# Strassen's products in a channel mixer's gate and up projections, and the down projection's weight sums computed earlier

## The chip, the cores and the metric

The kernel runs on one core of a Trainium2 chip. A core has a matrix engine (PE, with its weight loads shown apart as PEld), three engines for elementwise work (DVE, the vector engine; ACT, the scalar engine, which computes activation functions; POOL, GpSimd) and SP, which here only issues transfers. Each engine runs its own list of instructions strictly in order and waits on semaphores for the others. The metric is the device time of one execution in microseconds (us); the kernel before takes 1001.63 us in the median of three runs (1001.45 to 1002.13).

## The reference

The kernel is one layer of a streaming encoder block on x of 512 tokens by 1024 channels, in float32:

```python
h = rmsnorm(x, norm1_w)
proj = h @ w_in                       # q, k, v, z, b, a, glu, gates
o = gated_delta_rule_chunked(q, k, v, g, beta)
out_a = (rmsnorm(o, dn_norm_w) * silu(z)) @ dn_w_o
c = silu(layernorm(causal_depthwise_conv(glu_a * sigmoid(glu_b), cm_dw_w) + cm_dw_b))
out_b = c @ cm_w_pw2 + cm_b_pw2
x = x + (gate_a * out_a + gate_b * out_b) @ w_out
h2 = rmsnorm(x, norm2_w)
f_gate, f_up = split(h2 @ ffn_w_gate_up)      # 1024 -> 2 x 2816
x = x + (silu(f_gate) * f_up) @ ffn_w_down    # 2816 -> 1024
return rmsnorm(x, norm_f_w)
```

The change is in the last five lines, the channel mixer, and in the two output projections before it (`dn_w_o`, `cm_w_pw2`, then `w_out`).

## The kernel before, in words

**Split products.** To hold float32 accuracy on PE, every matrix is held as a high part (rounded to PE's float32r type) and a low part (the rest), and every product is three matmuls: high x high, high x low, low x high. `unit` loads 128 x 1024 weights (`raw`) on SP's queue, ACT makes the high part (`whi`, L102) and DVE the low part by a subtraction (`wlo`, L104). All three tiles have three buffers. `split3` issues the three matmuls (L113), `col_tile` one column tile of 128 outputs over all 512 tokens: 8 blocks of the inner dimension x 3 matmuls of 512 columns.

**Order.** A scheduler lays each engine's instructions out from the program text, the engines' modelled costs and the buffers that come free; what results is one fixed list for each engine.

**Output projections.** After the mixers, `ln_mean` (L560 to 573) makes the layer norm's variance sum: ACT squares eight tiles and POOL adds them up in `sacc` (L572, seven additions); `ln_norm` (L575) multiplies that sum by a matrix of ones on PE (L577) and goes on from there. The eight column tiles of `dn_w_o` run around it, `ln_norm` standing behind the third, then the eight of `cm_w_pw2`, then `tok_mm` for `w_out`, whose end is the second norm (`norm2`: ACT squares, POOL adds and takes the root, L786 and L788; DVE scales; PE transposes into `hh` and `hl`, the split activations).

**Gate and up.** For each of 22 hidden tiles f, `col_tile` runs twice (gate, up), ACT takes Silu (L871), DVE multiplies (`fm`, L878). For f < 11 POOL also runs `sums(f)` (L850): it loads a 128 x 4 x 512 piece of the down weights on its own queue, makes Strassen's four weight sums (L854 to L857) in place and stores them to DRAM (`wsum`). The activations' sums for the down projection are made by DVE at L888 to L892.

**Down projection.** It is already Strassen's (in Winograd's form): seven products of halves, in three calls of `two` (11 steps of 12 matmuls) and a last single product (L981 to L1006), whose weights are split by `unit` in groups of two; the final norm's work (`norm_f`) is issued between the third call and the last product.

## Time and profile before

One profiled execution took 998.75 us, 997.0 us of it from the first to the last instruction.

| | |
|---|---|
| median of three runs | 1001.63 us |
| profiled execution, its span | 998.75 us, 997.0 us |
| mean granted PE clock | 0.989 of full |
| PE, DVE, ACT, POOL busy | 96%, 68%, 52%, 29% of the span |
| output projections up to the second norm | about 476 to 640 us |
| gate and up | about 633 to 875 us |
| down projection and final norm | 875 to 997 us |

How the views are read. A row of groups gives line, engine, operation, tiles written and read, the shape and the count, then busy time, mean nanoseconds of one, and the idle time before them with what ended it. A row of the timeline gives start and length in us, and in brackets how long its engine had idled and for whom. A row of the table by stage gives a stretch, its length, and for each engine its busy time and instructions, then PE's granted clock, the share of time that the DMA engines were busy and GB/s. A row of the chain of waits gives start, length and what stood on it. Matmuls are pipelined: the length of one in the records is longer than the distance between two starts, which is what counts for throughput.

### The profile page before, as it was taken

Reading aid. Unit: us, or ns where it says so; the run is one execution under the profiler, and the core shown is the slowest. Engines: PE = TensorE matmul, PEld = TensorE weight load, DVE = VectorE, ACT = ScalarE, POOL = GpSimd, SP = SyncE. Lnnn points to the kernel's source line nnn. Section 1 sums busy time; section 2 is a strip of 40 time slices with the busy share of each in tenths; the row PEclk is TensorE's granted clock in tenths of the full one; section 3 lists DMA queues with packets and bytes.
Section 4 is the critical chain, followed back from the end, with each engine's and each line's share of the span. In section 5 each row is a group of like instructions: output and inputs, shape, how many; then the busy total and the mean of one; then the engine's idle time right before and its main releaser. Section 6 shows DMA issues by size and latency. Waiting matters only on the chain.

```text
span 997.0 us, 13416 instructions
## 1 busy us (share of the span) xinstructions
PE 961.6 (96%) x4775; PEld 791.6 (79%) x4775; DVE 673.7 (68%) x1044; ACT 515.4 (52%) x1057; POOL 292.6 (29%) x410
## 2 busy tenths in 40 slices
PE   7999799999999999999999999999999999999995
PEld 5687678788878888888888888888888888888784
DVE  4879699898779759898486644643444554468963
ACT  6697477777868675543456322422222222356543
POOL 0323845265452542000040000144342432001412
PEclk9999899999999999999999999999999999999997
DMA  9233313223142131233844432356656565256462
GB/s 318 85 114 97 98 54 106 80 74 105 43 118 76 59 102 64 85 128 137 273 128 156 137 120 85 119 210 220 231 179 239 195 232 183 92 168 190 158 212 85
DMA packets 48291, 138.50 MB, mean 139 GB/s; under 512 B 7472, under 2 KB 9424, under 8 KB 45408
## 3 DMA queue, kind: packets, MB, share of 16 engines
q1 hardware_dynamic: 44016, 112.36, 34.1%
q0 software_dynamic: 3488, 24.17, 6.9%
q10 hardware_dynamic: 720, 1.11, 0.3%
q8 instruction: 37, 0.61, 0.3%
q14 instruction: 30, 0.25, 0.1%
HBM read 119.52 MB, written 18.10 MB: 138 GB/s over the span
## 4 chain that ended last, share of the span: by engine, by line
PE 82%; DVE 6%; ACT 4%; POOL 4%; issue 2%; DMA 1%; SPq 0%; POOLq 0%; ACTq 0%; DVEq 0%
PE mm L113 62%; PE w L113 11%; DVE cv L543 2%; DVE wlo L104 1%; POOL Un L349 1%; PE b L414 1%; PE g L312 1%; ACT whi L102 1%; PE sp L487 1%; PE g L345 1%; ACT Un L348 1%; PE b L420 1%; PE st L494 1%; PE st L482 1%; PE b L438 1%
## 5 line engine op out<-in xcount | busy, mean ns | idle before, releaser
L102 ACT ACTIVATE whi<-raw 128x1024 fp32r<-128x1024 f32 x167 | 176.4, 1057 | 315.5 <-PE mm L113 180.5
L113 PE MATMUL mm<-hh,whi 128*128 128x512 f32 x816 | 327.5, 402 | 0.0
L113 PE MATMUL mm<-hl,whi 128*128 128x512 f32 x816 | 322.4, 395 | 2.3 <-POOL hl L228 1.6
L113 PE MATMUL mm<-hh,wlo 128*128 128x512 f32 x816 | 322.0, 395 | 0.7 <-DVE wlo L104 0.7
L104 DVE TENSOR_TENSOR wlo<-raw,whi 128x1024 fp32r<-128x1024 f32 x167 | 218.1, 1306 | 115.1 <-ACT whi L102 114.3
L543 DVE SCALAR_TENSOR_TENSOR cv<-c,c31w,cv 128x512 f32<-128x512 f32 x240 | 179.7, 771 | 2.0
L113 PEld LDWEIGHTS mm<-hl,whi 128*128 128x128 f32 x816 | 154.1, 189 | 33.1 <-POOL hl L228 2.9
L113 PEld LDWEIGHTS mm<-hh,wlo 128*128 128x128 f32 x816 | 154.0, 189 | 32.2 <-DVE wlo L104 1.1
L113 PEld LDWEIGHTS mm<-hh,whi 128*128 128x128 f32 x816 | 154.2, 189 | 29.9 <-ACT hh L227 0.2
L375 POOL TENSOR_TENSOR ytm<-U,y 128x60 f32<-128x60 f32 (+14 forms) x120 | 51.0, 425 | 62.1 <-DMA U<-sc 44.7
L299 DVE SCALAR_TENSOR_TENSOR acc<-mm,c4w,acc 128x511 f32<-128x511 f32 (+2 forms) x72 | 53.2, 740 | 9.9 <-ACT acc L296 9.2
L878 DVE TENSOR_TENSOR fm<-mm,fsg 128x512 f32<-128x512 f32 x21 | 14.5, 691 | 65.7 <-PE mm L113 65.7
L377 POOL TENSOR_TENSOR y<-y,ytm 128x60 f32<-128x60 f32 (+14 forms) x120 | 50.9, 424 | 9.3
L113 PE MATMUL mm<-yh,whi 128*128 128x512 f32 x128 | 50.6, 396 | 0.0
L113 PE MATMUL mm<-yh,wlo 128*128 128x512 f32 x128 | 49.8, 389 | 0.0
L113 PE MATMUL mm<-yl,whi 128*128 128x512 f32 x128 | 49.8, 389 | 0.0
L113 PE MATMUL w<-whi,fh 128*128 128x512 f32 (+1 forms) x115 | 45.3, 395 | 2.8 <-ACT whi L102 2.8
L113 PE MATMUL w<-wlo,fh 128*128 128x512 f32 (+1 forms) x115 | 45.6, 397 | 2.4 <-DVE wlo L104 2.4
L113 PE MATMUL w<-whi,fl 128*128 128x512 f32 (+1 forms) x115 | 45.0, 393 | 0.0
L786 POOL TENSOR_SCALAR ss<-ss 128x1 f32<-128x1 f32 x17 | 5.7, 336 | 128.8 <-ACT sg L784 116.2
L339 POOL TENSOR_TENSOR ss<-ss,root 128x4 f32<-128x4 f32 x8 | 10.3, 1291 | 85.5 <-DVE ss L337 85.5
L915 POOL TENSOR_TENSOR A<-A,u 128x512 f32<-128x512 f32 x4 | 6.2, 1574 | 97.1 <-ACT u L946 70.6
(288 smaller groups left out, 1511.2 us busy)
## 6 DMA issues: line engine op xcount, KB each, us to landing
raw<-in_win_dram SPq DMA_DIRECT2D x61, 512.0 KB, 3.3
raw<-in_wgu_dram SPq DMA_DIRECT2D x44, 512.0 KB, 3.4
wst<-in_wdn_dram POOLq DMA_DIRECT2D x11, 1024.0 KB, 6.0
wsum<-wst POOLq DMA_DIRECT2D x11, 1024.0 KB, 4.9
raw<-wsum SPq DMA_DIRECT2D x44, 256.0 KB, 3.4
raw<-in_wdn_dram SPq DMA_DIRECT2D x33, 256.0 KB, 2.9
A<-in_x_dram SPq DMA_DIRECT2D x8, 512.0 KB, 6.8
U<-sc SPq DMA_DIRECT2D x64, 64.0 KB, 3.1
```

What stands on the lines that cost most here:

```text
L102: marked(S.activation(hi[:, 0:n], raw[:, 0:n], AF.Copy), "unit")
L104: marked(V.tensor_tensor(out=lo[:, 0:n], in0=raw[:, 0:n], in1=hi[:, 0:n].bitcast(F32), op=ALU.subtract), "unit")
L113: marked(PE.matmul(ps, l, r, start=first and i == 0, stop=last and i == 2))
L299: marked(V.scalar_tensor_tensor(out=acc[:, s:], in0=ps[:, :T - s], scalar=c4w[:, j, k:k + 1], in1=acc[:, s:], op0=ALU.mult, op1=ALU.add))
L312: PE.transpose(ps[:, n, :], src[:, n, :], ident)
L339: G.tensor_tensor(out=nk, in0=kk, in1=root4, op=ALU.pow)
L345: PE.matmul(ps[:, n, :], kT[:, n, :], kT[:, n, :], start=True, stop=True)
L348: S.activation(Un[:, n, :], ps[:, n, :], AF.Copy, scale=nb2[:, n:n + 1])
L375: G.tensor_tensor(out=tm[:, :, 0:w], in0=U[:, k, :, k + 1:], in1=y[:, :, k:k + 1].broadcast_to([P, NT, w]), op=ALU.mult)
L377: G.tensor_tensor(out=y[:, :, k + 1:], in0=y[:, :, k + 1:], in1=tm[:, :, 0:w], op=ALU.add)
L543: V.scalar_tensor_tensor(out=acc, in0=c[:, k:k + T], scalar=c31w[:, i, k:k + 1], in1=acc, op0=ALU.mult, op1=ALU.add)
L878: V.tensor_tensor(out=fm, in0=pu, in1=sg, op=ALU.mult)
```

## The change

**Gate and up by Strassen's seven products.** The first two hidden tiles stay as they are. For each further one, `pair(f)` takes the gate and the up column tile together as a 2 x 2 block matrix (inner dimension in halves, gate and up the other way) against the activations in halves of inner dimension and tokens. It runs seven products of 4 x 3 = 12 matmuls of 256 columns. Besides the products of w = [a11, a12] as loaded, and of a22 (`w22`), it needs the sums s3 = a11 - a21, a22 := a21 + a22, a11 := a22 - a11, a12 := a12 - a11, all made by POOL, the last three in place in the loaded tiles `ra` and `rb`. `ws` is the split of the changed `ra`, `w3` that of s3, `w1` that of the changed a22. The outputs are put together from the four PSUM tiles z by DVE (`u`, `v`, `cw`, `fm`). The activations' sums are made once. `operands(f)` makes the down projection's operands; two subtractions of it go from DVE to POOL.

**Weight sums earlier.** The generator `sums` works in halves of 256 columns with two buffers, a step behind each column tile of the output projections and in `tok_mm`, the rest ahead of the end of that stage.

**What goes with it.** y1 is stored to DRAM and loaded again for the down projection (`ysp`, `y2`), the hidden tiles from 11 on are spilled to DRAM (`spill`) and loaded again in `set_3`. The sets of the down projection are made two steps later in `two`, and the final norm's work is spread between the steps of the last product.

```diff
     ...
+    def wsplit(raw, pool=None):
+
+        n = raw.shape[-1]
+        hi, lo = ((pool or wp).tile([P, n if pool else 1024], F32R, name=x)[:, 0:n] for x in ("whi", "wlo"))
+        marked(S.activation(hi, raw, AF.Copy), "unit")
+        marked(V.tensor_tensor(out=lo, in0=raw, in1=hi.bitcast(F32), op=ALU.subtract), "unit")
+        return hi, lo
+
 ...
+    FK = FF // 2
+    wsum = [dram.tile([P, 4, T], F32, name="wsum", bufs=FK) for _ in range(FK)]
+
+    def sums():
+        for k in range(FK):
+            for c in (slice(0, T // 2), slice(T // 2, T)):
+                r = sp2.tile([P, 4, T // 2], F32, name="wst")
+                nc.gpsimd.dma_start(r, a["wdn"][k].rearrange("p (i c) -> p i c", i=4)[:, :, c])
+                b11, b12, b21, b22 = (r[:, i, :] for i in range(4))
+                G.tensor_tensor(out=b11, in0=b12, in1=b11, op=ALU.subtract)
+                G.tensor_tensor(out=b12, in0=b22, in1=b12, op=ALU.subtract)
+                G.tensor_tensor(out=b22, in0=b22, in1=b11, op=ALU.subtract)
+                G.tensor_tensor(out=b21, in0=b22, in1=b21, op=ALU.subtract)
+                nc.gpsimd.dma_start(wsum[k][:, :, c], r)
+                yield
+
+    summing = sums()
 ...
         col_tile(ps, a["wo"][j], oh, ol)
+        next(summing, None)
         ma = mp.tile([P, T], F32, name="ma", bufs=KD + 1)
 ...
         col_tile(ps, a["wpw"][j], yh, yl)
+        next(summing, None)
         mb = tp.tile([P, T], F32, name="acc4")
 ...
                 for n in range(NT):
                     part(n, kp2, w)
+                next(summing, None)
 ...
         if hf:
+            nc.scalar.dma_start(ysp[n], y1[:, n, :])
 ...
     tok_mm("wout", KD, mh, ml, norm2, transposes)
+    for _ in summing:
+        pass
 ...
-    def sums(k):
-        r = fp.tile([P, 4, T], F32, name="wst", bufs=1)
-        nc.gpsimd.dma_start(r, a["wdn"][k].rearrange("p (i c) -> p i c", i=4))
-        b11, b12, b21, b22 = (r[:, i, :] for i in range(4))
-        G.tensor_tensor(out=b11, in0=b12, in1=b11, op=ALU.subtract)
-        G.tensor_tensor(out=b12, in0=b22, in1=b12, op=ALU.subtract)
-        G.tensor_tensor(out=b22, in0=b22, in1=b11, op=ALU.subtract)
-        G.tensor_tensor(out=b21, in0=b22, in1=b21, op=ALU.subtract)
-        nc.gpsimd.dma_start(wsum[k], r)
 ...
+    def sub(out, in0, in1, eng=G, op=ALU.subtract):
+        eng.tensor_tensor(out=out, in0=in0, in1=in1, op=op)
 ...
+    def operands(f):
+        if f < FK:
+            set1.append(xset())
+            hi, lo = (t[:, t1] for t in set1[f])
+            xsplit(hi, lo, fms[f][:, t1])
+            return
+        b, fm = fms[f - FK], fms[f]
+        s1 = fq.tile([P, TH], F32, name="s1")
+        sub(s1, b[:, t2], fm[:, t2], V, ALU.add)
+        hi, lo = (t[:, t2] for t in set1[f - FK])
+        xsplit(hi, lo, s1)
+        sub(b[:, t2], b[:, t1], b[:, t2])
+        sub(b[:, t1], s1, b[:, t1])
+    def spill(f):
+        spills.append(dram.tile([P, T], F32, name="fsp", bufs=FK))
+        nc.scalar.dma_start(spills[-1], fms[f])
 ...
+    xb = {}
+    for i, (ks, ts, eng) in enumerate(((kl, t1, V), (kl, t2, V), (kh, t2, G), (kh, t1, G))):
+        xb[i] = fx.tile([P, KH, TH], F32, name="xb%d" % i)
+        sub(xb[i], hh[:, ks, ts].bitcast(F32), hl[:, ks, ts].bitcast(F32), eng, ALU.add)
+    b11, b12, b22, b21 = (xb[i] for i in range(4))
+    sub(b11, b12, b11, V)
+    sub(b12, b22, b12, G)
+    sub(b22, b22, b11, V)
+    sub(b21, b21, b22, V)
+    T2, T3, T4 = ([fq.tile([P, KH, TH], F32R, name="%s%d" % (n, i), bufs=1) for n in ("th", "tl")] for i in range(3))
+    xsplit(*T4, b21)
+    xsplit(*T2, b22)
+    xsplit(*T3, b12)
+    B11, B21, B22 = ([t[:, ks, ts] for t in (hh, hl)] for ks, ts in ((kl, t1), (kh, t1), (kh, t2)))
+    T1 = [t[:, kl, t2] for t in (hh, hl)]
+    def hprod(ps, w, i, x):
+        for k in range(KH):
+            s = slice(i * T + k * P, i * T + k * P + P)
+            split3(ps, (w[0][:, s], w[1][:, s]), x[0][:, k, :], x[1][:, k, :], k == 0, k == KH - 1)
+    def pair(f):
+        ra = wp.tile([P, 1024], F32, name="raw")
+        rb = we.tile([P, 1024], F32, name="raw")
+        nc.sync.dma_start(ra, a["wgu"][f])
+        nc.sync.dma_start(rb, a["wgu"][FF + f])
+        z = [bank() for _ in range(4)] if f % 2 == 0 else [bank(), bank2(), bank2(), bank2()]
+        w = wsplit(ra)
+        w22 = wsplit(rb[:, T:], we)
+        hprod(z[0][:, t1], w, 0, B11)
+        hprod(z[1][:, t1], w, 1, B21)
+        hprod(z[2][:, t1], w22, 0, T4)
+        a11, a12, a21, a22 = (r[:, i * T:i * T + T] for r in (ra, rb) for i in range(2))
+        s3 = we.tile([P, T], F32, name="s3", bufs=1)
+        sub(s3, a11, a21)
+        sub(a22, a21, a22, G, ALU.add)
+        sub(a11, a22, a11)
+        sub(a12, a12, a11)
+        ws = wsplit(ra)
+        hprod(z[0][:, t2], ws, 0, T2)
+        cw = fq.tile([P, T], F32, name="cw")
+        S.copy(out=cw[:, t1], in_=z[0][:, t1])
+        u = fq.tile([P, TH], F32, name="cu")
+        sub(u, cw[:, t1], z[0][:, t2], V, ALU.add)
+        hprod(z[1][:, t2], ws, 1, B22)
+        w3 = wsplit(s3, we)
+        hprod(z[3][:, t1], w3, 0, T3)
+        v = fq.tile([P, TH], F32, name="cv2")
+        sub(v, u, z[3][:, t1], V, ALU.add)
+        w1 = wsplit(rb[:, T:])
+        if f == 2:
+            xsplit(*T1, b11)
+        hprod(z[2][:, t2], w1, 0, T1)
+        sub(cw[:, t2], u, z[2][:, t2], V, ALU.add)
+        fm = hidden(f)
+        sub(fm.rearrange("p (i t) -> p i t", i=2), z[2].rearrange("p (i t) -> p i t", i=2),
+            v.rearrange("p (a t) -> p a t", a=1).broadcast_to([P, 2, TH]), V, ALU.add)
+        sub(cw, cw, z[1], V, ALU.add)
+        S.activation(cw, cw, AF.Silu)
+        sub(fm, fm, cw, V, ALU.mult)
+    ff = None
+    for f in range(2, FF):
+        pair(f)
+        if f - 1 >= FK:
+            spill(f - 1)
+        if ff is None:
+            fxs.close()
+            ff = ctx.enter_context(tc.tile_pool(name="ff", bufs=1))
+            operands(0)
+            operands(1)
+        operands(f)
+    spill(FF - 1)
 ...
-        fm = fp.tile([P, T], F32, name="fm", bufs=FF)
-        fms.append(fm)
-        V.tensor_tensor(out=fm, in0=pu, in1=sg, op=ALU.mult)
-        if f < FK:
-            sums(f)
-            set1.append(xset())
-            hi, lo = (t[:, t1] for t in set1[f])
-            xsplit(hi, lo, fm[:, t1])
-        else:
-            b = fms[f - FK]
-            s1 = fp.tile([P, TH], F32, name="s1")
-            V.tensor_tensor(out=s1, in0=b[:, t2], in1=fm[:, t2], op=ALU.add)
-            hi, lo = (t[:, t2] for t in set1[f - FK])
-            xsplit(hi, lo, s1)
-            V.tensor_tensor(out=b[:, t2], in0=b[:, t1], in1=b[:, t2], op=ALU.subtract)
-            V.tensor_tensor(out=b[:, t1], in0=s1, in1=b[:, t1], op=ALU.subtract)
 ...
+            if k > 1:
+                then(k - 2)
+        then(FK - 2)
+        then(FK - 1)
+    def set_2(k):
+        set2.append(xset())
+        xsplit(*set2[k], fms[k])
+    def set_3(k):
+        r = dp.tile([P, T], F32, name="rl", bufs=3)
+        nc.gpsimd.dma_start(r, spills[k])
+        set3.append(xset())
+        xsplit(*set3[k], r)
+        sub(fms[k][:, t1], r[:, t1], fms[k][:, t1])
 ...
+        if k < 2:
+            add(2 + k, c1, p4[k], op=ALU.subtract)
+            squares(0, 2 + k, c1)
+            squares(1, 2 + k, c2, True)
+        elif k < 4:
+            add(k - 2, c1, p2[k - 2])
+            for cs, eng in ((c1, nc.scalar), (c2, nc.sync)):
+                scaled_out(k, cs, eng)
+            first_half(k - 2)
```

The orders on the engines change in three places.

On DVE in gate-up, before (two hidden tiles; names carry buffer numbers, `wlo` with its `raw` and `whi` is a unit's low part, `fsg` the Silu, `fl` an operand's low part):

```order
L104 TENSOR_TENSOR wlo_6509<-raw_6505,whi_6507 128x1024
L878 TENSOR_TENSOR fm_6458<-mm_6395,fsg_6426 128x512
L104 TENSOR_TENSOR wlo_6554<-raw_6550,whi_6552 128x1024
L844 TENSOR_TENSOR fl_6468<-fm_6458,fh_6467 128x256
L104 TENSOR_TENSOR wlo_6586<-raw_6582,whi_6584 128x1024
L878 TENSOR_TENSOR fm_6535<-mm_6472,fsg_6503 128x512
```

And now, one pair. `raw_7043` and `raw_7044` are ra and rb of a pair n+1, `raw_7176` and `raw_7177` those of pair n+2, `cu_6985`, `cv2_7015`, `cw_6983`, `fm_7034` belong to pair n:

```order
L99 TENSOR_TENSOR wlo_7101<-raw_7043,whi_7100 128x1024
L886 TENSOR_TENSOR cv2_7015<-cu_6985,mm_6917 128x256
L886 TENSOR_TENSOR cw_6983<-cu_6985,mm_6916 128x256
L886 TENSOR_TENSOR fm_7034<-mm_6916,cv2_7015 128x512
L886 TENSOR_TENSOR cw_6983<-cw_6983,mm_6915 128x512
L99 TENSOR_TENSOR wlo_7133<-s3_7095,whi_7132 128x512
L99 TENSOR_TENSOR wlo_7151<-raw_7044,whi_7150 128x512
L886 TENSOR_TENSOR fm_7034<-fm_7034,cw_6983 128x512
L99 TENSOR_TENSOR wlo_7185<-raw_7176,whi_7184 128x1024
L883 TENSOR_TENSOR fl_7040<-fm_7034,fh_7039 128x256
L99 TENSOR_TENSOR wlo_7189<-raw_7177,whi_7188 128x512
L886 TENSOR_TENSOR cu_7118<-cw_7116,w_7047 128x256
```

Where DVE had three or four instructions for a tile, it now has twelve, and `ws` of pair n+1 (first row) stands ahead of the closing sums of pair n, and w22 of pair n+2 behind them.

On POOL in gate-up, before (one tile's weight sums between their transfers):

```order
L852 DMA wst_6306<-in_wdn_dram 128x2048
L854 TENSOR_TENSOR wst_6306<-wst_6306 128x512
L855 TENSOR_TENSOR wst_6306<-wst_6306 128x512
L856 TENSOR_TENSOR wst_6306<-wst_6306 128x512
L857 TENSOR_TENSOR wst_6306<-wst_6306 128x512
L858 DMA wsum_6167<-wst_6306 128x2048
```

And now (hidden tiles from 11 on; in each pair s3, two operand subtractions in fm, then a22, a11, a12):

```order
L886 TENSOR_TENSOR s3_8169<-raw_8117,raw_8118 128x512
L886 TENSOR_TENSOR fm_6471<-fm_6471 128x256
L886 TENSOR_TENSOR fm_6471<-s1_7974,fm_6471 128x256
L886 TENSOR_TENSOR raw_8118<-raw_8118 128x512
L886 TENSOR_TENSOR raw_8117<-raw_8118,raw_8117 128x512
L886 TENSOR_TENSOR raw_8117<-raw_8117 128x512
```

The four 512-column subtractions that no engine waited for in this stage are gone; the four in their place stand between a load and a split that PE waits for. The subtraction into `raw_8118` (a22) waits for DVE's low part of w22, which reads that place.

On POOL at the layer norm in the output projections, before:

```order
L736 DMA nw2_5419<-in_n2w_dram 128x1024
L572 TENSOR_TENSOR sacc_5012<-sacc_5012,acc4_5016 128x512
L572 TENSOR_TENSOR sacc_5012<-sacc_5012,acc4_5020 128x512
L572 TENSOR_TENSOR sacc_5012<-sacc_5012,acc4_5024 128x512
L572 TENSOR_TENSOR sacc_5012<-sacc_5012,acc4_5028 128x512
```

And now (`wst_5324` and `wst_5366` are the fifth and the sixth half of the weight sums):

```order
L734 DMA wsum_5063<-wst_5324 512x1x256
L730 TENSOR_TENSOR wst_5366<-wst_5366 128x256
L578 TENSOR_TENSOR sacc_5015<-sacc_5015,acc4_5019 128x512
L731 TENSOR_TENSOR wst_5366<-wst_5366 128x256
L578 TENSOR_TENSOR sacc_5015<-sacc_5015,acc4_5023 128x512
L732 TENSOR_TENSOR wst_5366<-wst_5366 128x256
L578 TENSOR_TENSOR sacc_5015<-sacc_5015,acc4_5027 128x512
L733 TENSOR_TENSOR wst_5366<-wst_5366 128x256
L578 TENSOR_TENSOR sacc_5015<-sacc_5015,acc4_5031 128x512
L734 DMA wsum_5063<-wst_5366 512x1x256
L578 TENSOR_TENSOR sacc_5015<-sacc_5015,acc4_5035 128x512
L728 DMA wst_5408<-in_wdn_dram 128x4x256
```

Ahead of the first row stand the five halves' loads, sums and stores; the weight sums are now woven into the seven additions. On PE the ones-matmul of `ln_norm` keeps its place.

More of the change, by code (lines that the diff above doesn't have):

```diff
@@ L750, in block_kernel @@
         V.tensor_tensor(out=ml[j], in0=mb, in1=mh[j].bitcast(F32), op=ALU.subtract)
+    ysp = [dram.tile([P, D], F32, name="ysp", bufs=NT) for _ in range(NT)]
     def tok_mm(wname, kts, xh, xl, post, between):
@@ L869, in block_kernel @@
             k_loop(*first[0], slice(2 * P, T))
-        sg = fp.tile([P, T], F32, name="fsg")
+        sg = fq.tile([P, T], F32, name="cw")
         S.activation(sg, pg, AF.Silu)
@@ L895, in block_kernel @@
+    ff = None
[10 more added lines that the diff above has]
+    spill(FF - 1)
+    fqs.close()
     hps.close()
     dp = ctx.enter_context(tc.tile_pool(name="dp", bufs=2, side="right"))
+    nfw = dp.tile([P, D], F32, name="nfw", bufs=1)
+    nc.gpsimd.dma_start(nfw, a["nfw"].partition_broadcast(P))
@@ L914, in add @@
     def add(n, cs, what, op=ALU.add, eng=V):
[L915 removed]
+        eng.tensor_tensor(out=y2[:, n, cs], in0=y2[:, n, cs], in1=what, op=op)
     def prods(w, i, x, j, accs, first, last):
@@ L1005, in block_kernel @@
         add(1, cs, ps)
-        norm_f(4 if c else 1, 1, cs)
+        squares(4 if c else 1, 1, cs, c)
+        if not c:
+            out(0)
+    out(1)
 def _layout(i):
```

119 lines of the change are left out of this document (58 added, 61 removed).

## The prediction

> **What bounds the kernel now.** I read the page's busy times first, then the table by stage, then the chain of waits.
>
> ```profile
> PE 961.6 (96%) x4775; PEld 791.6 (79%) x4775; DVE 673.7 (68%) x1044; ACT 515.4 (52%) x1057; POOL 292.6 (29%) x410
> ```
> ```profile
> core 0: us, PE busy (x) PEld busy (x) DVE busy (x) ACT busy (x) POOL busy (x), PEclk, DMA share, GB/s
> 476.00:516.00 40.00, 40.00 (x175) 32.27 (x174) 25.88 (x27) 20.26 (x30) 13.03 (x8) 1.00 0.63 212
> 516.00:587.00 71.00, 71.00 (x315) 58.76 (x314) 45.82 (x57) 31.17 (x40) 0.00 (x0) 1.00 0.46 144
> 647.20:700.00 52.80, 52.80 (x234) 43.72 (x233) 19.86 (x20) 14.55 (x20) 21.69 (x18) 1.00 0.62 216
> ```
> ```profile
> 647.16 228.28 PE mm L113 x1007
> ```
>
> In the output projections (476 to 587) and in gate-up (647.2 to 875.4) PE is busy all the time at full clock, DVE and POOL are not. The chain holds gate-up as one unbroken run of matmuls: 228.28 us / 1007 = 0.2267 us for a 512-column matmul, so 48 x 0.2267 = 10.88 us for one pair of column tiles. Whatever the change does, time there is gained only by less PE work, and lost once another engine needs over 10.88 us per pair.
>
> **Part 1, the matmuls.** Each of 20 pairs goes from 48 matmuls of 512 columns to 7 x 12 = 84 of 256. The program before has 256-column matmuls at the end of the norm:
>
> ```profile
> 642.08 0.28 PE L113 MATMUL w<-hh,whi 128*128 128x256 f32 x1
> ...
> 644.00 0.28 PE L113 MATMUL w<-hl,whi 128*128 128x256 f32 x1
> ```
>
> Sixteen starts lie between these two: 1.92 / 16 = 0.120 us, a little over half of 0.2267. So a pair is 84 x 0.120 = 10.08 us of PE. All that PE can give is 20 x 0.80 = 16 us.
>
> **Part 2, who feeds these products.** Prices of the other engines, alone:
>
> ```profile
> 647.27 0.69 DVE L878 TENSOR_TENSOR fm<-w,fsg 128x512 f32<-128x512 f32 x1 [0.58 <-PE w L113]
> 648.17 1.23 DVE L104 TENSOR_TENSOR wlo<-raw,whi 128x1024 fp32r<-128x1024 f32 x1 [0.21 <-ACT whi L102]
> 649.32 0.42 DVE L844 TENSOR_TENSOR fl<-fm,fh 128x256 fp32r<-128x256 f32 x1
> ```
> ```profile
> 650.37 1.29 POOL L854 TENSOR_TENSOR wst<-wst 128x512 f32<-128x512 f32 x1 [8.25 <-DMA wst<-in_wdn_dram]
> 651.73 1.29 POOL L855 TENSOR_TENSOR wst<-wst 128x512 f32<-128x512 f32 x1
> ```
> ```profile
> L102 ACT ACTIVATE whi<-raw 128x1024 fp32r<-128x1024 f32 x166 | 175.9, 1060 | 315.5 <-PE mm L113 180.5 <-issue 89.0 <-PE w L113 36.9
> ```
>
> DVE: 1.23, 0.69 and 0.42 us for 1024, 512 and 256 columns; one starts 0.08 before the record of the last ends (649.32 against 648.17 + 1.23), which makes 1.15, 0.62 and 0.35 from start to start. POOL: 1.29 us for 512 columns, 1.36 from start to start. ACT: 1.06 us for a 1024-column split.
>
> The orders shown above close a ring in which each link waits for the one before, once per pair. From the start of DVE's low part of the summed weights (ws) of pair n+1: ws 1.15; u+z3 and the two gate halves 0.35 + 0.35; fm 0.62; cw 0.62; low part of s3 0.62, of the last weight quarter 0.62; the product fm x cw 0.62; low part of w of pair n+2 1.15; fl 0.35; low part of w22 of pair n+2 0.69 with its end. That is 7.1 us. Only then may POOL overwrite a22, because w22 was split from that place; a22, a11, a12 are 3 x 1.36 = 4.1. Then ACT splits the sum (1.06), and DVE may start the next ws: 7.1 + 4.1 + 1.06 and some 0.1 of handing over = 12.4 us. Behind the waiting ws stand on DVE the closing sums of pair n and all splits of later pairs, on ACT the same splits and Silu, on PE the ws products of the next pair. So the ring sets the pace, not DVE's total.
>
> POOL also has s3 of pair n+2 to do, which becomes free in the middle of DVE's stretch. What that costs is seen here:
>
> ```profile
> 702.31 2.36 DVE L104 TENSOR_TENSOR wlo<-raw,whi 128x1024 fp32r<-128x1024 f32 x1 [0.15 <-ACT whi L102]
> 704.60 1.51 DVE L844 TENSOR_TENSOR fl<-fm,fh 128x256 fp32r<-128x256 f32 x1
> ```
> ```profile
> 702.30 1.29 POOL L854 TENSOR_TENSOR wst<-wst 128x512 f32<-128x512 f32 x1 [4.52 <-DMA wst<-in_wdn_dram]
> 703.67 2.15 POOL L855 TENSOR_TENSOR wst<-wst 128x512 f32<-128x512 f32 x1
> ```
>
> POOL began at 702.30 and kept 1.29; DVE's split, one hundredth later, took 2.36 = 1.23 + 1.13; POOL's next took 2.15 while DVE finished. The two alternate. So s3 adds about 1.1: **13.5 us a pair**. From tile 11 on, `operands` adds to DVE s1 (in place of u+z3, which moves ahead of ws) and to POOL two 256-column subtractions, of which no row shows the length: half of 1.29 from below, 1.29 from above; I take 0.73, nearer to half, since every POOL row has a fixed part. Both fall on splits that need the same inputs: 2 x 0.73, **15.0 us a pair**. Bounds: 12.4 (nothing collides) and 1 us more each (every handing over collides).
>
> The Trainium skill's page "SBUF — State Buffer", section "SBUF: two separate sides", says that GpSimd and a VectorE instruction with two SBUF inputs lock each other out for a whole instruction. By it a pair costs 13.5 and 15.0, without it 12.4; the rows at 702.3 agree with it.
>
> The first ring can start once pair 2 has run. Until then PE is fed from ahead: tile 1 10.9, pair 2 10.1, three products of pair 3 4.3. DVE's and POOL's sums of the activations (some 8 DVE instructions of 1.23) lie under tile 1; I add 0.5 because one now stands ahead of the last `hl`. Then nine rings of 13.5 and nine of 15.0, 256.5, and the last pair's ws and four products, 1.15 + 5.8. Sum 289.3 against 228.3: **+61 us**. With the lower bound 18 x 12.4 = 223, +28; with the upper +79.
>
> **Part 3, the moved weight sums.** They leave gate-up, where POOL's time was free, and go to POOL's stream behind 476.72, ahead of and between work that PE waits for:
>
> ```profile
> 476.72 0.63 POOL L736 DMA_DIRECT2D nw<-in_n2w_dram  x1 [26.91 <-PE b L312]
> 502.04 12.87 POOL L572 TENSOR_TENSOR sacc<-sacc,acc 128x512 f32<-128x512 f32 x7 [24.69 <-ACT acc L571]
> ```
> ```profile
> L577 PE MATMUL mm<-sacc,cst x2: 592/618/644, 515.0 to 515.5; 128*128 128x512 f32 x2
> ...
>   POOL sacc L572: 0.2, 1
> ```
> ```profile
> raw<-in_wgu_dram SPq DMA_DIRECT2D x44, 512.0 KB, 3.4
> wst<-in_wdn_dram POOLq DMA_DIRECT2D x11, 1024.0 KB, 6.0
> wsum<-wst POOLq DMA_DIRECT2D x11, 1024.0 KB, 4.9
> ```
>
> The seven sacc additions end at 502.04 + 12.87 = 514.91, and PE's ones-matmul of the layer norm (L577) starts at 515.0; the view of that line shows that PE sat 0.2 us before it until POOL's sacc came: no slack. In the new order five halves of the sums and one subtraction of the sixth stand before the first sacc, three subtractions and three transfers between them. Each half needs its load, four subtractions and its store, and with two buffers a load waits for the store two halves back. For 512 KB on POOL's queue no row stands; bounds 3.4 (SP's 512 KB) and 6.0 / 4.9 (POOL's 1 MB); I take 5 and 4.2, and 0.8 from start to start of a 256-column subtraction. Loads at 476.7 land at 481.7; eight subtractions to 488.1; stores land at 492.3; loads land at 497.3; two halves with their stores end at 504.8; of the next two loads the second holds POOL until the store before it has landed, 508.4; the fifth half ends at 513.0, its store's issue and the sixth's first subtraction at 514.4: sacc starts 12.4 us late. Then 12.9 for sacc as before, 3 x 0.8 and 3 issues of about 0.55: end at 531.3, **16 us late** (9 and 22 by the two bounds). Behind L577 stands all of PE, and 516 to 587 is full, so nothing is caught up. After a stall of this size the clock falls:
>
> ```profile
> 977.85 0.50 PE L113 MATMUL w<-whi,fh 128*128 128x512 f32 x1 [2.83 <-ACT whi L102]
> ...
> 979.93 0.80 PE L113 MATMUL w<-wlo,fh 128*128 128x512 f32 x1 [1.35 <-DVE wlo L104]
> 980.52 0.63 PE L113 MATMUL w<-whi,fh 128*128 128x512 f32 x1
> 980.95 0.63 PE L113 MATMUL w<-whi,fl 128*128 128x512 f32 x1
> ...
> 985.43 0.40 PE L113 MATMUL w<-wlo,fh 128*128 128x512 f32 x1
> 985.66 0.39 PE L113 MATMUL w<-whi,fh 128*128 128x512 f32 x1
> ```
>
> In these rows of the last product, after two gaps, matmuls start 0.43 apart until 985.43 and 0.23 apart behind it: some 5.4 us at half pace, 2.7 lost. So part 3 costs **+18.7**. The 16 halves left take about 12.6 us for two by the same prices, until 628 to 639, and the second norm's roots stand behind them on POOL:
>
> ```profile
> 620.21 0.58 POOL L788 TENSOR_TENSOR ss<-ss,half 128x1 f32<-128x1 f32 x1
> ```
>
> The first of these was at 620.2 and is now due at 639: just free, bounds 0 and +10.
>
> **Part 4, down projection.** The matmuls stay. Reloading y2 and the spilled tiles is hidden by the first pair of products:
>
> ```profile
> 875.44 30.60 PE w L113 x135
> ```
>
> It runs 30.6 us before y2 is added to; a late transfer would cost its own 5 or 6. In the rows of the last product PE lost 2.8 + 1.35 us waiting for its fourth split, which stands behind norm work, and 2.7 to the clock. With that norm work spread between matmuls I give back 6 of these 6.9 (bounds 0 and all, with 1 or 2 of small gaps ahead): **-6**.
>
> **Sum** against the profiled execution, 997.0 of span and 998.75 in all: 998.75 + 61 + 18.7 - 6 = 1072.5. It lies 2.9 below the median of the runs, 1001.63; so I predict **1075 us**.
>
> **Rivals.** *PE sets the pace* (faster). If the ring closes in under 10.08 us, only PE counts: -16 and -6, with the sums hidden: 1001.6 - 22 = 980. For it: PE at 96% and four other engines with room. Against: it needs the ring 3.4 us shorter than the rows say, and even without any collision it is 12.4, over the 10.88 of before. 8%. *No collisions and short transfers*: rings of 12.4, sacc 9 late: +28 + 11.7 - 6, 1035. The rows at 702.3 speak against half of it. 17%. *The sums also end late for the second norm*, and collisions lengthen them: each us past 639 is one of PE; with +10 there and rings 0.5 longer, 1075 + 19 = 1094. DVE is busy 45.8 of 71 us there, which speaks for it. 13%. *Nothing changes*: gains and losses cancel; 2%. My forecast 60%.
>
> From these, slower by over 0.2% (what a measurement of this kernel can tell) 0.90, faster 0.08, within it 0.02. The range reaches to both slower rivals: 1032 to 1102; the 980 case is left out.
>
> **What would show it.** The pace of a pair: 13.5 us early and 15 late in gate-up, with PE idle 3 to 5 us in each, ended by the split of ws, and that by POOL's a12. PE's wait for sacc at the layer norm, 9 to 22 us, and matmuls 0.43 apart behind it. The last product without gaps. The prediction is wrong if gate-up runs at 10 to 11 us a pair, or if sacc starts at 502 as before.

## The result, and the profile after

The changed kernel takes **1110.93 us** in the median of four runs (1108.98 to 1113.42), the kernel before 1001.72 beside it: a ratio of 1.107, 95% interval 1.105 to 1.110. It is slower, as forecast, but by 109 us where the forecast was 73, and the time lies 9 us above the range. The profiled execution has a span of 1107.7 us, 110.7 more than that of before.

To see where they went I cut both executions at the same four places. These are single rows of PE's timeline, of the kernel before and of the changed one: the second matmul of the output projections, the second 256-column matmul at the second norm's end, the first of the down projection, and the last one of all.

```profile
498.88 0.39 PE L113 MATMUL mm<-yl,whi 128*128 128x512 f32 x1
...
633.07 0.28 PE L113 MATMUL w<-hl,whi 128*128 128x256 f32 x1
...
875.28 0.39 PE L113 MATMUL w<-whi,fh 128*128 128x512 f32 x1
...
988.97 0.28 PE L113 MATMUL mm<-wlo,fh 128*128 128x256 f32 x1
```
```profile
503.64 0.39 PE L118 MATMUL mm<-yl,whi 128*128 128x512 f32 x1
...
682.13 0.28 PE L118 MATMUL w<-hl,whi 128*128 128x256 f32 x1
...
985.78 0.40 PE L118 MATMUL w<-whi,fh 128*128 128x512 f32 x1
...
1100.18 0.28 PE L118 MATMUL mm<-wlo,fh 128*128 128x256 f32 x1
```

| stretch | before, us | after, us | difference | forecast |
|---|---|---|---|---|
| up to the output projections | 498.9 | 503.6 | +4.8 | 0 |
| output projections and second norm | 134.2 | 178.5 | **+44.3** | +18.7 |
| gate and up | 242.2 | 303.7 | **+61.4** | +61 |
| down projection, to the last matmul | 113.7 | 114.4 | **+0.7** | -6 |
| behind it | 8.0 | 7.5 | -0.5 | 0 |
| span | 997.0 | 1107.7 | +110.7 | +73.7 |

The first row is put down to scatter and not to the change: in the eleven kernels below, nearly all of them with the same code up to there, the first cut lies anywhere from 499.3 to 503.1. The next three rows are the change's.

**Output projections.** From the view of who waited for whom, two of PE's lines from 440 us on in the changed kernel (us in total, times, longest):

```profile
PE mm L583 <- POOL sacc L578: 23.9, 1, 23.9
...
PE mm L849 <- DVE xs L830: 15.6, 1, 15.6
```

PE waits twice for a norm that waits for POOL: 23.9 us for the layer norm's additions (`sacc`), and 15.6 at the second norm (`xs` needs POOL's root). Behind the first wait the matmuls start 0.43 us apart for a while, as the prediction's rows had shown it for the last product. What POOL does ahead of the two, from its timeline:

```profile
481.50 1.61 POOL L728 DMA_DIRECT2D wst<-in_wdn_dram  x2 [26.93 <-PE b L318]
...
488.44 0.93 POOL L730 TENSOR_TENSOR wst<-wst 128x256 f32<-128x256 f32 x1 [4.79 <-DMA wst<-in_wdn_dram]
...
497.38 1.50 POOL L734 DMA_DIRECT2D wsum<-wst  x2
504.30 0.78 POOL L728 DMA_DIRECT2D wst<-in_wdn_dram  x1 [5.43 <-DMA wsum<-wst]
...
530.35 1.33 POOL L578 TENSOR_TENSOR sacc<-sacc,acc 128x512 f32<-128x512 f32 x1
...
604.05 0.78 POOL L728 DMA_DIRECT2D wst<-in_wdn_dram  x1
...
620.26 0.78 POOL L728 DMA_DIRECT2D wst<-in_wdn_dram  x1
...
666.52 0.74 POOL L734 DMA_DIRECT2D wsum<-wst  x1 [0.30 <-POOL wst L733]
...
668.90 0.58 POOL L820 TENSOR_TENSOR ss<-ss,half 128x1 f32<-128x1 f32 x1
```

The first load lands 6.9 us after its issue, the first store 6.9 after its own. From 604.05 to 620.26, one round of two halves, 16.2 us pass. The last store is issued at 666.52, and the roots come right behind it, at 668.90 (before: 620.21).

**Gate and up.** The pace is that of one ring per pair. DVE's, ACT's and POOL's timelines for one ring of the early pairs, and the table by stage for eight early and eight late rings:

```profile
780.36 1.23 DVE L99 TENSOR_TENSOR wlo<-raw,whi 128x1024 fp32r<-128x1024 f32 x1 [4.88 <-ACT whi L98]
...
784.56 1.77 DVE L886 TENSOR_TENSOR fm<-fm,cw 128x512 f32<-128x512 f32 x1
...
787.73 0.68 DVE L99 TENSOR_TENSOR wlo<-raw,whi 128x512 fp32r<-128x512 f32 x1
...
793.66 1.23 DVE L99 TENSOR_TENSOR wlo<-raw,whi 128x1024 fp32r<-128x1024 f32 x1 [4.92 <-ACT whi L98]
```
```profile
788.49 4.05 POOL L886 TENSOR_TENSOR raw<-raw 128x512 f32<-128x512 f32 x3 [2.70 <-DVE wlo L99]
```
```profile
792.57 1.06 ACT L98 ACTIVATE whi<-raw 128x1024 fp32r<-128x1024 f32 x1 [5.00 <-POOL raw L886]
```
```profile
core 0: us, PE busy (x) PEld busy (x) DVE busy (x) ACT busy (x) POOL busy (x), PEclk, DMA share, GB/s
740.53:846.78 106.25, 92.07 (x672) 88.56 (x672) 67.11 (x96) 39.00 (x65) 44.30 (x32) 0.92 0.25 80
861.58:977.44 115.86, 96.34 (x672) 92.48 (x672) 79.88 (x105) 38.97 (x65) 63.80 (x48) 0.88 0.26 87
```

From ws to ws: DVE's own work up to the split of w22 (787.73), POOL's three sums 4.05, ACT's split 1.06, and DVE starts again after 13.30. Eight early rings take 106.25, 13.28 each, eight late ones 115.86, 14.48 each. What is longer in a late ring, DVE's rows and POOL's beside them:

```profile
912.17 0.96 DVE L883 TENSOR_TENSOR fl<-s,fh 128x256 fp32r<-128x256 f32 x1
913.05 1.22 DVE L99 TENSOR_TENSOR wlo<-raw,whi 128x512 fp32r<-128x512 f32 x1
```
```profile
911.19 1.65 POOL L886 TENSOR_TENSOR fm<-fm 128x256 f32<-128x256 f32 x1 [1.09 <-DVE s L886]
```

Beside POOL's two operand subtractions, the first of which is this row and the second starts at 912.92, `fl` takes 0.96 us, where early rings have 0.41, and the split of w22 1.22, where the early row above has 0.68.

### The profile page after: what moved, and what is told of

Read it like the earlier page. It is cut to its first block, busy times and chain, and to the rows that moved or that the text cites. A ratio compares the mean times of both kernels' runs of the same rounds, so it can differ in the third digit from the quotient of the medians.

```text
span 1107.7 us, 15461 instructions
## 1 busy us (share of the span) xinstructions
PE 986.1 (89%) x5495; PEld 839.5 (76%) x5495; DVE 780.3 (70%) x1182; ACT 554.4 (50%) x1139; POOL 482.5 (44%) x605
## 4 chain that ended last, share of the span: by engine, by line
PE 40%; POOL 18%; DVE 15%; DMA 12%; issue 8%; ACT 7%; SPq 0%; POOLq 0%; ACTq 0%; DVEq 0%
PE mm L118 25%; POOL raw L886 7%; DVE wlo L99 7%; DMA wst<-in_wdn_dram 6%; PE w L118 6%; ACT whi L98 3%; DVE fm L886 2%; DMA raw<-wsum 2%; DMA wsum<-wst 2%; POOL wst L731 2%; POOL wst L732 2%; DVE fl L883 2%; POOL wst L733 1%; POOL wst L730 1%; DVE cv L549 1%
## 5 line engine op out<-in xcount | busy, mean ns | idle before, releaser
L118 PE MATMUL mm<-hh,whi 128*128 128x512 f32 (+1 forms) x616 | 240.5, 391 | 0.0
L118 PE MATMUL mm<-hl,whi 128*128 128x512 f32 (+1 forms) x616 | 234.8, 381 | 2.3 <-POOL hl L234 1.6
L118 PE MATMUL mm<-hh,wlo 128*128 128x512 f32 (+1 forms) x616 | 234.3, 380 | 1.3 <-DVE wlo L99 1.3
L886 POOL TENSOR_TENSOR raw<-raw 128x512 f32<-128x512 f32 x60 | 78.9, 1316 | 48.3 <-DVE wlo L99 45.2
L118 PE MATMUL w<-th,whi 128*128 128x256 f32 x160 | 51.2, 320 | 26.5 <-ACT whi L98 26.5
L118 PE MATMUL w<-hh,wlo 128*128 128x256 f32 x232 | 69.8, 301 | 3.6 <-DVE wlo L99 3.5
L118 PE MATMUL w<-hl,whi 128*128 128x256 f32 x232 | 68.8, 297 | 1.0 <-DVE hl L852 1.0
L118 PE MATMUL w<-hh,whi 128*128 128x256 f32 x232 | 68.9, 298 | 0.2 <-ACT hh L851 0.2
L118 PE MATMUL w<-th,wlo 128*128 128x256 f32 x160 | 52.8, 330 | 13.0 <-DVE wlo L99 12.9
L118 PEld LDWEIGHTS w<-hh,wlo 128*128 128x128 f32 x232 | 47.8, 206 | 5.1 <-DVE wlo L99 4.6
```

Of the source, the lines that this page charges most:

```text
L118: marked(PE.matmul(ps, l, r, start=first and i == 0, stop=last and i == 2))
L886: eng.tensor_tensor(out=out, in0=in0, in1=in1, op=op)
```

## The experiments

All beside the kernel before on the same chip; a number in brackets behind a time is the ratio to it with its 95% interval.

**The weight sums left out.**

```diff
-    summing = sums()
+    summing = iter(())
...
-    two(lambda k: (wd(k, 0), wsum[k][:, 0, :]), set1, p1 + p5, set_2)
+    two(lambda k: (wd(k, 0), wd(k, 1)), set1, p1 + p5, set_2)
...
```

(The two other calls of `two` read plain weights in the same way.)

> The changed kernel with the down weights' sums left out (no loads, subtractions and stores of them; the down projection reads the plain weights in their place, so its output is not the reference's). Theory (the sums on POOL hold up the two norms): both waits of PE, 23.9 us before the layer norm's ones-matmul and 15.6 before the second norm's transposes, fall below 1 us, and with them the half clock behind each (2.3 and 1.3): 24.7 + 2.3 + 16.0 + 1.3 = 44 less, about 1067 us. Rival 1 (POOL's additions are late because ACT's squares or DVE are): PE's waits stay, 1111. Rival 2 (the sums' 23 MB of transfers also slow the weight loads elsewhere): more than 44, 1055 or less.

Measured: 1061.9 us (1.062, 1.059 to 1.064), 49 less. Neither norm's line is left among PE's waits from 500 to 650 us:

```profile
PE w L118 <- DVE hl L852: 1.0, 1, 1.0
PE w L118 <- DVE wlo L99: 0.3, 1, 0.3
PE w L118 <- ACT hh L851: 0.2, 1, 0.2
```

The stretch from the output projections to the second norm takes 134.2 us, exactly that of before. So all its 44.3 us come from the sums; ACT's squares and DVE do not delay PE without them. The other 5 us are near the scatter of the first stretch (its cut is 2.9 earlier here).

**Three buffers for the sums.**

```diff
-PAD4 = 506
+PAD4 = 480
...
-    sp2 = ph2.enter_context(tc.tile_pool(name="sp2", bufs=2))
+    sp2 = ph2.enter_context(tc.tile_pool(name="sp2", bufs=3))
```

> The changed kernel with three buffers instead of two for the halves of the weight sums (a filler tile made smaller to fit), nothing left out. Theory (with two buffers a load waits for the store two halves back, so two halves take one round trip of 15.3 us): three halves per round trip, 5.1 us each, not far above POOL's own 4 x 0.8 + 2 x 0.75 = 4.7; the 22 halves end near 613 instead of 666.5, PE's second wait (15.6) goes, the first shrinks from 23.9 to some 13: 1111 - 17 - 11 = 1083 us. Rival (the transfers' bandwidth or POOL's own work sets the pace): halves stay 7.6 us apart, 1111.

Measured: 1089.94 us (1.090, 1.087 to 1.093). PE's second wait is gone, as the theory has it. The first is 18.6 us where 13 was expected, and POOL reaches the second norm at 639.68, not 613: a third buffer makes the round less short than I had worked out.

**The sums ordered behind the layer norm's additions.**

```diff
+                with tc.issue_after(last_sq[0]) if 2 * k + (c.start > 0) >= 3 else ExitStack():
                     r = sp2.tile([P, 4, T // 2], F32, name="wst")
...
```

(`last_sq` is the last of the seven additions. The three buffers of the run before are kept.)

> The changed kernel with three buffers for the weight sums, the first three halves ahead of the layer norm's additions (sacc) on POOL, all later ones ordered behind the last of these; nothing left out. Theory (PE's two waits are POOL's place in line and the round trips, nothing else): sacc starts at about 502 to 505 and PE's first wait falls below 2 us; the 19 halves left take 6.1 us each (from the run with three buffers) and end near 515 + 116 = 631 plus what the run is late, before the second norm's roots at about 640; so about what leaving the sums out gave, 1064 us. Rival (transfers alone hold the sums to 7.6 us a half): they end at 660, PE waits 15 to 20 us at the second norm, 1085.

Measured: 1098.04 us (1.095, 1.092 to 1.097): a miss of the theory's time (1064), and 13 us beyond the rival's (1085). The first wait is gone and the second is back, 18.6 us. POOL's rows:

```profile
503.61 8.42 POOL L580 TENSOR_TENSOR sacc<-sacc,acc 128x512 f32<-128x512 f32 x5 [5.35 <-ACT acc L579]
...
516.44 2.29 POOL L731 DMA_DIRECT2D wst<-in_wdn_dram  x3
...
651.79 0.73 POOL L737 DMA_DIRECT2D wsum<-wst  x1 [0.30 <-POOL wst L736]
```

19 halves from 516.44 to 652.5 are 7.2 us each. Whichever comes first in POOL's line, the other norm waits: at this pace the sums do not fit between the two.

**Their loads on SP's queue,** on top of that.

```diff
-                    nc.gpsimd.dma_start(r, a["wdn"][k].rearrange("p (i c) -> p i c", i=4)[:, :, c])
+                    nc.sync.dma_start(r, a["wdn"][k].rearrange("p (i c) -> p i c", i=4)[:, :, c])
```

> As the run with the sums behind sacc (three buffers, three halves ahead), but the loads of the halves are issued on SP's queue instead of POOL's. Theory (POOL's list, in which a load's issue waits for a store and with it holds back subtractions whose data have landed, sets the 7.2 us a half): POOL then has 4 x 0.81 + 0.3 + 0.75 = 4.3 us a half, the 19 halves left end near 515 + 19 x 4.4 = 599, neither wait of PE is left: 1062 to 1064 us. Rival (the load, the sums and the store of one buffer follow each other, 6 + 4.3 + 5 = 15.3 us, three buffers give 5.1, and loads that wait on SP's queue hold back the weight loads behind them): sums end at 612, no second wait, but new waits of PE for weights of 5 to 15 us in all: 1070 to 1080.

Measured: 1098.62 us (1.098, 1.095 to 1.101). The rival is right, and worse than it said. The sums now take 5.2 us a half and end at 618, no norm waits, and PE stands for weights instead. The largest of SP's own waits from 515 to 650 us (us in total, times, longest), then ACT's and PE's timelines:

```profile
SPq L731 <- DMA wsum<-wst: 66.0, 15, 10.7
```
```profile
561.03 1.06 ACT L98 ACTIVATE whi<-raw 128x1024 fp32r<-128x1024 f32 x1 [20.39 <-DMA raw<-in_wpw_dram]
```
```profile
562.66 0.80 PE L118 MATMUL mm<-yh,whi 128*128 128x512 f32 x1 [12.01 <-ACT yh L750]
```

A load for the sums (L731) that waits for a free buffer, 66.0 us in all, stands ahead of the projections' weights on SP's queue. ACT waits 20.4 us at a weight split for such weights, the splits of the activations stand behind it, and PE waits 12.0 for these. The stretch takes 167.9 us against 134.2.

**The pair's sums left out.**

```diff
-        s3 = we.tile([P, T], F32, name="s3", bufs=1)
-        sub(s3, a11, a21)
-        sub(a22, a21, a22, G, ALU.add)
-        sub(a11, a22, a11)
-        sub(a12, a12, a11)
...
-        w3 = wsplit(s3, we)
+        w3 = wsplit(a21, we)
```

> The changed kernel with POOL's four weight sums per pair left out (the same splits and products run on the weights as loaded, so the output is not the reference's). Ring theory: nothing then waits for POOL, DVE needs 7.3 us a pair and ACT 5, so PE's 10.1 us set the pace; 18 pairs save 3.2 early and 4.4 late, 68 us: about 1043 us, no wait of PE for the split of the summed weights. Rival (DVE and the order of its work set the pace, POOL only adds collisions): the pace stays at 12 us or more, 1075 or above.

Measured: 1035.3 us (1.034, 1.030 to 1.037), 76 less where 68 were expected. The splits of w and of ws alternate 4.39 and 5.69 us apart for all eighteen pairs: 10.08 us a pair, PE's own 84 x 0.120, and PE has no wait between 720 and 910 us. The whole stretch takes 229.0 us. So 13.3 us below the kernel before is what the seven products would give if their sums cost nothing, against the 16 at most that the prediction had for it.

**The same sums, off the ring.**

```diff
-        sub(a22, a21, a22, G, ALU.add)
-        sub(a11, a22, a11)
-        sub(a12, a12, a11)
+        sub(s3, a21, a22, G, ALU.add)
+        sub(s3, a22, a11)
+        sub(s3, a12, a11)
...
-        w3 = wsplit(s3, we)
+        w3 = wsplit(a21, we)
```

> The changed kernel in which POOL does the same four operations per pair from the same loaded tiles, but writes them all to one scratch tile that nobody reads; splits and products run on the weights as loaded (the output is not the reference's). POOL's work and its use of SBUF stay, nobody waits for it but the loads. Ring theory: only collisions with DVE's instructions that read two SBUF tiles are left, 5.0 us of DVE and 5.4 of POOL a pair, so 10.4 early and 11.5 to 12 late: 18 pairs save about 2.8 each, 50 us, 1060. Rival (collisions, with whatever DVE does, are the price: 7.3 + 5.4 = 12.7 early and 14 late): 0.5 a pair saved, 1101.

Measured: 1051.79 us (1.052, 1.048 to 1.055), the stretch 247.1; about 10.1 us a pair early, 11.3 late. POOL's and DVE's timelines show the collisions alone:

```profile
741.61 6.62 POOL L886 TENSOR_TENSOR s<-raw 128x512 f32<-128x512 f32 x4 [4.50 <-DMA raw<-in_wgu_dram]
```
```profile
742.21 1.78 DVE L99 TENSOR_TENSOR wlo<-raw,whi 128x1024 fp32r<-128x1024 f32 x1 [0.52 <-ACT whi L98]
...
745.95 0.68 DVE L886 TENSOR_TENSOR fm<-w,cv 128x512 f32<-128x512 f32 x1
...
747.14 1.64 DVE L99 TENSOR_TENSOR wlo<-raw,whi 128x512 fp32r<-128x512 f32 x1
```

While POOL is at work, a split that reads two tiles in SBUF takes 1.78 instead of 1.23 us, or 1.64 instead of 0.68; the sum with one operand in PSUM (`w`) keeps its 0.68. This bears out, for these three shapes, the rule of the Trainium skill that the prediction named ("SBUF — State Buffer", section "SBUF: two separate sides"). But collisions do not set the early pace: with POOL's full work and no ring, PE does. Of the 13.28 us some 3.2 are the ring's.

**Separate tiles for the sums.** A version of the last that computes everything:

```diff
+        r1 = wr.tile([P, T], F32, name="r1", bufs=2)
+        rs = wr.tile([P, 1024], F32, name="rs")
+        sub(r1, a21, a22, G, ALU.add)
+        sub(rs[:, 0:T], r1, a11)
+        sub(rs[:, T:], a12, rs[:, 0:T])
         s3 = we.tile([P, T], F32, name="s3", bufs=1)
         sub(s3, a11, a21)
-        sub(a22, a21, a22, G, ALU.add)
-        sub(a11, a22, a11)
-        sub(a12, a12, a11)
-        ws = wsplit(ra)
+        ws = wsplit(rs)
...
-        w1 = wsplit(rb[:, T:])
+        w1 = wsplit(r1)
```

> The changed kernel in which the pair's sums go to tiles of their own (the changed a22 with two buffers, a11 and a12 with one) instead of over the loaded weights, s3 last of the four; nothing left out. Ring theory: without the overwriting, POOL no longer waits for the split of w22; pace as in the run with the sums off the ring, 10.1 to 10.5 early and 11.4 late: 1052 us. Rival (the single-buffered tile of a11 and a12 closes a new ring: ws 1.2, then two sums under collisions 4, ACT's split 1.1, and s3's turn 3.5, with what DVE does between): 12 early and 13 late, 1085.

Measured: 1053.65 us (1.051, 1.048 to 1.054), the ring theory's number. Six early pairs and five late ones in the table by stage, columns as above:

```profile
747.43:808.62 61.19, 61.19 (x512) 61.19 (x511) 61.19 (x74) 31.22 (x49) 34.91 (x24) 1.00 0.30 104
841.96:899.64 57.68, 51.67 (x422) 50.65 (x421) 57.51 (x67) 23.88 (x40) 41.47 (x30) 1.00 0.34 114
```

Early: PE busy all the time at full clock, 10.2 us a pair, and DVE, lengthened by collisions, just as full. Late: DVE full, PE not, 11.5 us a pair. The wait that made the ring was the overwriting of a loaded tile. (The same edit puts s3 last of the four; what that does by itself was not run.)

**The operand subtractions back on DVE,** on top of that.

```diff
-        sub(b[:, t2], b[:, t1], b[:, t2])
-        sub(b[:, t1], s1, b[:, t1])
+        sub(b[:, t2], b[:, t1], b[:, t2], V)
+        sub(b[:, t1], s1, b[:, t1], V)
```

> The changed kernel with the pair's sums in tiles of their own, as before, and the two operand subtractions of tiles 11 on given back to DVE. Theory (late pairs are slower by POOL's two subtractions of 256 columns, 0.74 each, that lie on DVE's time, while DVE does the same in 0.34): late pace 11.4 - 2 x 0.4 = 10.6, 9 pairs: 7 us less than the run with separate tiles, 1046 us. Rival (DVE's own added work is what makes late pairs slow): 11.4 or more, 1054.

Measured: 1051.01 us (1.050, 1.048 to 1.053); late pairs take 11.3, not 10.6. The table by stage for five late pairs:

```profile
847.47:904.02 56.55, 51.68 (x422) 50.66 (x422) 56.20 (x76) 23.91 (x41) 29.28 (x20) 1.00 0.34 117
```

DVE is as full as before, and the pace is nearer to the rival's: what bounds the late pairs is DVE's list, its own work and the collisions together. With the two subtractions on POOL, `fl` took 0.95 us in the late pairs and the split of w22 1.23, now they take 0.42 and 0.69; the 1.1 us won is mostly spent again on the two subtractions themselves, 0.35 each from start to start.

**The reload issued later.**

```diff
-    nc.gpsimd.dma_start(nfw, a["nfw"].partition_broadcast(P))
...
-    for n in range(NT):
-        nc.gpsimd.dma_start(y2[:, n, :], ysp[n])
...
     def set_2(k):
+        if k % 2 and k < 8:
+            nc.sync.dma_start(y2[:, k // 2, :], ysp[k // 2])
...
+    nc.sync.dma_start(nfw, a["nfw"].partition_broadcast(P))
```

> The changed kernel with the reloads of y2 (4 x 512 KB) issued between the weights of the first pair of products on SP's queue, steps 1, 3, 5 and 7, and the last norm's weights behind it, instead of all on POOL's queue at the start. Theory (these 2.5 MB share the DMA engines with the first weights and delay them): PE's gaps in the first pair of products, some 5 us in all beyond steady spacing, go: 4 to 5 less, 1106 us. Rival (the gaps come from DVE's and ACT's new order there): no change, 1111; second rival (in line on SP's queue they delay the weights as much): no change either, with the gaps later.

Measured: 1110.9 us (1.107, 1.105 to 1.110), no change. In the changed kernel PE's waits in the down projection stand at two places, here the first of the one and the first of the other:

```profile
1006.13 0.50 PE L118 MATMUL w<-whi,fh 128*128 128x512 f32 x1 [1.13 <-ACT whi L98]
...
1058.87 0.50 PE L118 MATMUL w<-wlo,fh 128*128 128x512 f32 x1 [1.56 <-DVE wlo L99]
```

With the later reload there is no wait left before 1020 us, and the first eight quarters of the down weights land 4.0 us after their issue in the median instead of 5.4: the theory is right on the cause. But the wait at the second place grows:

```profile
1060.70 0.79 PE L118 MATMUL w<-wlo,fh 128*128 128x512 f32 x1 [3.42 <-DVE wlo L99]
```

The stretch gets 1.1 us shorter (113.3), which the time of the whole does not show.

**The norm's spreading alone, on the kernel before.**

```diff
...
         for n in range(2):
             part(k, n, p3[n], 0, T, k == 0, n == 1 and k == K0 - 1)
+        if k < 2:
+            add(2 + k, c1, p4[k], op=ALU.subtract)
+            squares(0, 2 + k, c1)
+            squares(1, 2 + k, c2, True)
+        elif k < 4:
+            add(k - 2, c1, p2[k - 2])
+            for cs, eng in ((c1, nc.scalar), (c2, nc.sync)):
+                scaled_out(k, cs, eng)
+            first_half(k - 2)
...
```

> The kernel before with one part of the change alone: the final norm's work spread between the steps of the last product, as in the changed kernel (y1 stays in SBUF). Theory of the prediction: the waits of 2.8 and 1.35 us in the last product and the half clock behind them (2.7) go, 6 less: 995.5 us. Rival (the additions that now stand ahead of the first splits of that product delay these instead, as the waits of 1.6, 0.7 and 0.6 at the same place in the changed kernel suggest): 2 to 4 of the 6 are lost again, 998 to 1000.

Measured: **995.04 us** (992.23 to 997.44), ratio 0.992, 0.990 to 0.994: the theory's time, and 0.8% faster than the kernel before. The waits of PE in the down projection, of the kernel before and of this one:

```profile
PE w L113 <- ACT whi L102: 2.8, 1, 2.8
PE w L113 <- DVE wlo L104: 2.4, 3, 1.4
```
```profile
PE w L113 <- DVE wlo L104: 1.1, 2, 0.7
```

The stretch takes 106.5 us against 113.7.

**All of it mended at once.** The sums behind `sacc` with three buffers and loads on SP's queue, separate tiles, the operand subtractions on DVE, the reload between the weights.

> All of it, nothing left out: sums behind sacc with three buffers and loads on SP's queue, the pair's sums in separate tiles, operand subtractions on DVE, y2's reload between the weights. Theory: the stretches add: 134 us from the layer norm to the second norm as in the kernel before, gate-up 239 (before 242), down projection 113 (before 114): 998 us, about the kernel before. Rival (the parts collide: the loads on SP's queue or SBUF's layout cost new waits): 1010 to 1030.

Measured: 1035.86 us (1.035, 1.032 to 1.038), the rival, and 6 us beyond its range. Gate and up takes 245.5 us (before 242.2), the down projection 113.7 (113.7, where the spreading alone gave 106.5), the output projections 170.0 (134.2). Nearly all that is left of the loss is the place of the weight sums. A kernel with separate tiles and the sums left in gate and up was not run.

## Why the prediction was right or wrong

**What bounds the kernel, part 1: right.** A pair's products cost PE 10.08 us, to the hundredth, once nothing else stops it. The gain at stake was even smaller than the 16 us given as the most: 13.3.

**Part 2, the ring: right in mechanism and place, the sum in part by luck.** Forecast 13.5 and 15.0 us a pair, measured 13.28 and 14.48; the links are those named, ended by ACT's split of ws, that by POOL's sums, these by DVE's split of w22. The collision of s3 was put at 1.1: the product fm x cw takes 1.77 instead of 0.68. That the stretch came to +61.4 for +61 is luck: two terms were off and cancel. Eighteen rings came to about 250 instead of 256.5, start-up and end to about 40 instead of 32.8, where gaps of 1.3 us in tile 1 and 3.0 in the first pair were not seen. That the ring, and not collisions, is the price is shown by the runs off the ring (10.1 to 11.5 us with all of POOL's work). The late term, 1.5, came to 1.2, and the rows of a late ring bear out what it was read from: two collisions, 0.55 and 0.54 us, where I had 0.73 each. Moving the two subtractions to DVE does not undo that where DVE's list is the bound: it gave 0.2 of 11.5.

**Part 3, the moved sums: the step that failed.** Wrong is the term "the 16 halves left take about 12.6 us for two" and with it "until 628 to 639 ... just free". From 539.51 to 654.53 seven rounds take 115 us, 16.4 each. The view of the sums' tile tells what stood in them (idle time of POOL before these rows, us and times):

```profile
  DMA wsum<-wst: 30.0, 12
  DMA wst<-in_wdn_dram: 29.8, 12
...
  POOL wst L733: 6.3, 19
...
DMA to landing us min/median/max: 3.3/5.0/9.1
```

My round had one load of 5 us, eight subtractions at 0.8 and about a microsecond. In the mean of the seven rounds 6.5 us pass from the issue of the first load to its first subtraction (most waits for a store, ahead of the second load, lie within these), the subtractions are longer, up to 1.8 us for one, and the two stores' issues take 0.75 each, with 0.30 that POOL stands before each. Eight rounds x 3.8 us = 30 us late. That lateness ate the slack I had counted on at the second norm: +17.3 (16.0 from start to start of PE, 1.3 of clock behind it), where I had 0 and a bound of +10. The mechanism was in the list, as the rival of 1094 us, but with "+10 there" as its price. The same landing times made `sacc` late: its first addition stands at 530.35, 23.5 later than before (502.04 + 4.8), where I had 12.4; PE's stall came to 24.7 for 16, beyond my bound of 22. The half clock behind it cost 2.3 for 2.7.

The bounds were at fault as well. I took 512 KB between the 3.4 us of SP's loads and the 6.0 and 4.9 of POOL's 1 MB, all from stretches of the kernel before, with the DMA engines busy 0.46 to 0.63 of the time. With the sums they are busy 0.75 of the time from 545 to 655 us, where the projections' weights take 5.8 and 6.3 us instead of 3.3; with the sums left out it is 3.4 in the same window. The change itself raised the price of SP's loads that I read from the kernel before. POOL's own loads land after 6.0 us in the median, my upper bound, and 9.1 at most.

**Part 4: right where it was made, given back elsewhere.** The spreading gives 7.2 us alone, and in the changed kernel too the last product has no gap. But "hidden by the first pair of products" does not hold for the reload: 2.5 MB at the start of the down projection make PE lose 5.0 us there, the price I named for the case and did not add, and some 3.7 us are lost at the third pair's start, where the kernel before lost 1.6. Moving the reload moves that loss.

**Rivals.** *PE sets the pace* fell with the ring. *No collisions and short transfers* was wrong in its second half above all: transfers became longer. What came is the third, *the sums also end late*, with 17.3 us at the second norm for its 10 and without its longer rings, together with the main case. The range ended at 1102 because that rival's own term was taken from one bound and not worked out.

## What to carry to other kernels

Work that is moved to an idle engine brings its transfers along: count the rounds of load, work and store with the landing times of the stretch it goes to, with the traffic that it adds, and ask for each thing behind it in that engine's list when it will come. A sum written over a loaded tile ties its engine to the last reader of that tile; a tile of its own took 57 us off here. And a change of several parts is worth taking apart: one of its parts, alone on the kernel before, was the one gain.

## What the runs showed of the hardware

- Three buffers in place of two, behind the layer norm's additions, took the sums only from 8.2 to 7.2 us a half while POOL issued the loads, and to 5.2 once SP did. POOL's list in order has a part in that: a load's issue that waits for a store holds back subtractions whose data are there. POOL's rows with three buffers, where the second one is the third subtraction of a half already begun:

```profile
497.41 0.80 POOL L728 DMA_DIRECT2D wst<-in_wdn_dram  x1 [3.48 <-DMA wsum<-wst]
498.23 0.75 POOL L732 TENSOR_TENSOR wst<-wst 128x256 f32<-128x256 f32 x1
```

- Issuing the loads on SP's queue also spares POOL 0.78 us a half, and they land after 5.4 us instead of 6.3. How the 2.0 us a half divide among these three is not shown.
- The mean granted clock fell to 0.92 and 0.88 in gate and up: matmuls run at half pace for some 3 us after part of the gaps (0.21 us apart at 256 columns from 965.08 to 968.29). It cost nothing in the early pairs: DVE never waited for PE there, its 29.4 us of idle time in six rings all end with ACT's split.
- The start of a kernel scatters by 3.8 us between executions of nearly the same code (499.3 to 503.1 at the first cut of the eleven kernels), about 0.4% of the time; comparing stretches removes it.
